# Five adds of squares in each feed forward's last group, from VectorE to GpSimd

## The chip, the cores and the metric

The kernel runs on one core of a Trainium2 chip. The core has five engines that work side by side and wait for each other by semaphores: TensorE (PE; matrix products, into the accumulator memory PSUM), VectorE (DVE), ScalarE (ACT), GpSimd (POOL), which also issues some of the DMAs, and SyncE (SP), which issues the others. The metric is the device time of one execution in microseconds (us), as the median of several runs; less is better.

## The reference, cut to what matters

One layer of a network over 512 positions and a width of 1024: a feed forward, a token mixer (attention) and a second feed forward, each behind an RMS norm, and a norm at the end.

```
def rmsnorm(x, g):
    x32 = x.astype(jnp.float32)
    y = x32 * lax.rsqrt(jnp.mean(x32 * x32, axis=-1, keepdims=True) + EPS)
    return (y * g.astype(jnp.float32)).astype(x.dtype)

def swiglu(x, w_gate, w_up, w_down):
    return (jax.nn.silu(x @ w_gate) * (x @ w_up)) @ w_down

x = x + 0.5 * swiglu(rmsnorm(x, ffn1_norm), ffn1_w_gate, ffn1_w_up, ffn1_w_down)
x = x + token_mixer(rmsnorm(x, mix_norm), w_in, w_out, ...)
x = x + 0.5 * swiglu(rmsnorm(x, ffn2_norm), ffn2_w_gate, ffn2_w_up, ffn2_w_down)
return rmsnorm(x, final_norm)
```

What the change touches is `mean(x32 * x32)`: the squares of x, summed over the width, which the norm of the mixer and the last norm need.

## The kernel before, in words

**Layout.** The activations lie transposed: x is eight tiles `x[0]` to `x[7]`, each of 128 of the 1024 columns (on the partitions) by 512 positions. All is float32. A product of two such matrices is made as three TensorE products of parts: each operand is split into a high part (a copy rounded to a shorter format, by ScalarE) and a low part (what the rounding left, a subtraction by VectorE), and high x high, high x low and low x high are added in PSUM (`mm3`, L123 to L126). So the weights also pass through ScalarE (`high`, L383) and VectorE (`low`, L387) before TensorE can use them.

**Squares.** `sq` (L90) is one tile of 128 x 512. It collects, over the eight tiles of x, the squares: the first tile's square is written to it, each of the others is squared into a scratch tile by ScalarE and then added to `sq`. TensorE later sums `sq` over the partitions (`means`, L177, and `final_means`, L1236). There are three places that add: `add_square` (L717, VectorE) at the start; `square_x` (L145, GpSimd, L151) after the mixer; and `squared` (L788, VectorE, L800) in the last group of both feed forwards, which is what changes.

**A feed forward** (`ffn`, L199) ends with its down product. Most of it is made by a recursive scheme of seven products for four blocks (`SEVEN`, L46), in units of two tiles of x. The last group's units are named ("d", 1, m) with m = 0, 2, 4, 6; each updates `x[m]` and `x[m+1]`. A unit has seven steps in the order a11, s3, s2, a12, s1, a22, s4, one product of twelve TensorE instructions each. `down_step` (L591) puts the updates of x from PSUM on VectorE (all printed as L424): s1 and s4 both use the bank `py`, s1's result being read by VectorE before s4 is added to it. For each step VectorE also makes a low part (L387), and for s2 and s4 a sum of weights (`total`, L365 and L367). The sums s1 and s3 of the weights are made by DMAs: SP loads one block, and GpSimd issues a DMA that adds the other (`weight_sums`, L331 to L340).

**Order.** In this stage the order of VectorE's, ScalarE's, GpSimd's and SP's instructions is fixed by hand: a list of events with due times in units of `STEP` (L55) is worked off in order of time (`pipeline`, L613), and each engine works its instructions off in that order. After steps a22 and s4 of a last group's unit, `ended` (L611) is called for x[m+1] and then x[m]. So x[1] comes first, then x[0], x[3], x[2], x[5], x[4], x[7], x[6]. In the first feed forward `ended` is `to_mixer` (L802): ScalarE makes the high part `xh`, then the square, and VectorE the add and the low part `xl` (L806), for the mixer's products. In the second it is `squared` alone, and the last unit (x[6], x[7]) goes another way (`last`, L1218; its squares are not added but summed by TensorE). So `squared` adds for m = 0, 2, 3, 4, 5, 6, 7 in the first feed forward and for m = 0, 2, 3, 4, 5 in the second: twelve adds; x[1] is squared straight into `sq`.

The scratch tiles `sqd` come from a pool of two buffers (tag "ptb", L796). Behind the first feed forward, some small work for the mixer is placed where there is room: a DMA on GpSimd's queue loads `lt` (L814), and VectorE reads it (L816); also the first weights of the mixer (L115, L116).

Of the kernel before, what the change touches and what calls it, by code (L numbers as in the profile page):

```python
# [18 lines left out]
ALU = mybir.AluOpType  # L19
# [35 lines left out]
STEP, PLAIN_STEP = 1410, 4080  # L55
# [10 lines left out]
def tile_macaron(ctx: ExitStack, tc, xs, xT, wf, wgu1, wst1, wd1, wdg1, wqk, wv, wo, wgu2, wst2, wd2,  # L66
                 wdg2, lams, relb, onehot, addc, out):
    nc = tc.nc
    V, A, G, T = nc.vector, nc.scalar, nc.gpsimd, nc.tensor
# [20 lines left out]
    sq = cp.tile([P, S], F32, tag="sq", name="sq")  # L90
# [697 lines left out]
    def squared(m, t, put):  # L788

        if m == 1:  # L790
            put(t + STEP, A.activation, sq[:], x[m], AF.Square)
            return
        sqt = {}

        def square():
            sqt[0] = tp.tile([P, S], F32, tag="ptb", name=f"sqd{m}")  # L796
            A.activation(sqt[0][:], x[m], AF.Square)

        put(t + STEP, square)
        put(t + 2 * STEP, lambda: V.tensor_tensor(sq[:], sq[:], sqt[0][:], op=ALU.add))  # L800

    def to_mixer(m, t, put):  # L802
        g = gain(1, m)
        put(t + STEP, lambda: A.activation(xh[m][:], x[m], AF.Copy, scale=g))
        squared(m, t, put)
        put(t + 2 * STEP, lambda: V.scalar_tensor_tensor(xl[m][:], x[m], g, xh[m][:].bitcast(F32),  # L806
                                                  op0=ALU.mult, op1=ALU.subtract))
# [33 lines left out]
    def put(t, rank, f, *a):  # L841
        at.setdefault(t, []).append((rank, f, a))
# [432 lines left out]
    def final_end():  # L1275
# [8 lines left out]
    means, spread = rstd("n3", n3)  # L1284
    ffn(wgu2, wst2, wd2, wdg2, EARLY[1], PAIRED[1], 2, early, n3, "b",
        {(0, 4): means, (0, 7): spread}, squared, last=last)


# [97 lines left out]
```

## Time and profile before

| what | us |
|---|---|
| median of 3 runs | 926.12 (926.03 to 926.28) |
| the profiled execution | 925.75 |
| its span, first to last instruction | 924.0 |
| TensorE busy | 911.2 |
| VectorE busy | 722.2 |
| ScalarE busy | 532.9 |
| GpSimd busy | 98.3 |
| the first feed forward's last group | 297.99 to 338.43 |
| the second feed forward's last group | 870.75 to 910.82 |

How to read the rows: PE, PEld, DVE, ACT, POOL and SP are the engines (PEld is TensorE's weight load). A row of a timeline has start (us from the span's start), duration in us, engine, line of the kernel, operation, output<-inputs by the program's names (buffer numbers left out), shapes and types, and how many instructions it stands for; in brackets the idle time of the engine before it and what ended it. In the names, a and b at the end stand for the first and the second feed forward (`pyda` is the bank y of a down unit of the first). The rows of instructions on one engine can overlap by some 0.08 us, since the next one is started while the last one ends; the time an instruction takes of a full queue is the distance from its start to the next start.

### The profile page before, as it was taken

What the parts mean: (1) busy time and instruction counts of PE and PEld (TensorE: products, weight loads), DVE (VectorE), ACT (ScalarE), POOL (GpSimd) and SP (SyncE); (2) the same over time, 40 slices, a digit from 0 to 9 for tenths busy, and PEclk for the clock granted to TensorE, in tenths of its full rate; (3) what the DMA queues carried; (4) which work ended last, traced back from release to release, by engine and by line L of the source; (5) the groups of instructions that cost most, each with busy time, mean ns of one, the idle gap of its engine ahead of it and who ended that gap; (6) DMA issues with size and microseconds to landing.
All of it is one profiled execution on the core that took longest, in us unless ns stands there. A gap on an engine that the chain in (4) does not pass through costs nothing.

```text
span 924.0 us, 17216 instructions
## 1 busy us (share of the span) xinstructions
PE 911.2 (99%) x6462; PEld 845.8 (92%) x6462; DVE 722.2 (78%) x1491; ACT 532.9 (58%) x1101; POOL 98.3 (11%) x117
## 2 busy tenths in 40 slices
PE   9999999999999999999999999999999999999995
PEld 7788999999999998988989888888999899999995
DVE  7697997687997994779764547697899678798796
ACT  7455774455764664666756655354676354667462
POOL 0011101012102100000000003201110102220100
PEclk9999999999999999999999999999999999999998
DMA  7176646578757732343333104445674757884732
GB/s 256 64 199 154 169 130 183 142 205 208 196 152 194 188 129 86 115 132 121 91 115 93 69 23 137 130 135 145 162 190 113 197 155 185 217 216 118 209 105 92
DMA packets 60388, 136.71 MB, mean 148 GB/s; under 512 B 6848, under 2 KB 9152, under 8 KB 60304
## 3 DMA queue, kind: packets, MB, share of 16 engines
q1 hardware_dynamic: 46304, 110.14, 36.2%
q0 software_dynamic: 14000, 25.47, 17.2%
q8 instruction: 50, 0.82, 0.4%
q14 instruction: 34, 0.28, 0.1%
HBM read 130.30 MB, written 2.14 MB: 143 GB/s over the span
## 4 chain that ended last, share of the span: by engine, by line
PE 93%; DVE 4%; ACT 1%; issue 1%; DMA 0%; SPq 0%; DVEq 0%; ACTq 0%
PE po L1052 2%; PE pv L902 2%; PE pv L904 2%; PE pv L903 2%; PE pwo L124 2%; PE pwo L125 2%; PE pwo L126 2%; PE pua L125 1%; PE pua L124 1%; PE pua L126 1%; PE pt L1036 1%; PE pda L125 1%; PE pdb L125 1%; PE pub L124 1%; PE pda L124 1%; PE pub L125 1%
## 5 line engine op out<-in xcount | busy, mean ns | idle before, releaser
L1015 DVE CUSTOM_DVE_ANT_0 pr<-sc,strip 128x128 f32<-128x128 f32 (+3 forms) x64 | 30.8, 487 | 30.6 <-PE sc L1013 30.2
L1018 ACT ACTIVATE pr<-pr,small 128x128 f32<-128x128 f32 (+3 forms) x64 | 36.0, 563 | 28.2 <-DVE small L1015 27.3
L383 ACT CAST w<-s2b 128x512 fp32r<-128x512 f32 x50 | 31.2, 625 | 20.6 <-DVE s2b L365 20.3
L383 ACT CAST w<-s2a 128x512 fp32r<-128x512 f32 x46 | 28.7, 625 | 21.7 <-DVE s2a L365 18.9
L151 POOL TENSOR_TENSOR sq<-sq,sqt 128x512 f32<-128x512 f32 x7 | 10.9, 1560 | 248.2 <-ACT sqt L150 248.2
L387 DVE TENSOR_TENSOR w<-s2b,w 128x512 fp32r<-128x512 f32 x50 | 34.4, 688 | 2.4 <-ACT w L383 2.0
L902 PE MATMUL pv<-w,xh 128*128 128x256 f32 x128 | 36.0, 281 | 0.0
L903 PE MATMUL pv<-w,xl 128*128 128x256 f32 x128 | 35.8, 280 | 0.0
L904 PE MATMUL pv<-w,xh 128*128 128x256 f32 x128 | 35.8, 280 | 0.0
L1052 PEld LDWEIGHTS po<-v,ptb 128*128 128x128 f32 x240 | 32.6, 191 | 2.5
L387 DVE TENSOR_TENSOR w<-s2a,w 128x512 fp32r<-128x512 f32 x46 | 31.6, 687 | 1.7 <-ACT w L383 1.3
L1052 PE MATMUL po<-v,ptb 128*128 128x64 f32 (+1 forms) x240 | 32.3, 268 | 0.0
L1042 ACT COPY ptb<-pt 128x128 f32<-128x128 f32 (+3 forms) x47 | 19.4, 420 | 16.4 <-PE pt L1036 16.0
L124 PE MATMUL pq<-xh,w 128*128 128x512 f32 x64 | 26.7, 416 | 0.0
L864 DVE TENSOR_TENSOR w<-raw_qk,w 128x512 fp32r<-128x512 f32 x32 | 21.7, 687 | 5.3 <-ACT w L860 5.3
L124 PE MATMUL pwo<-mh,w 128*128 128x512 f32 x64 | 25.6, 400 | 0.0
L125 PE MATMUL pq<-xl,w 128*128 128x512 f32 x64 | 25.1, 393 | 0.0
L124 PE MATMUL pk<-xh,w 128*128 128x512 f32 x64 | 25.1, 392 | 0.0
L126 PE MATMUL pq<-xh,w 128*128 128x512 f32 x64 | 25.1, 392 | 0.0
L125 PE MATMUL pwo<-ml,w 128*128 128x512 f32 x64 | 25.0, 391 | 0.0
L126 PE MATMUL pk<-xh,w 128*128 128x512 f32 x64 | 25.0, 391 | 0.0
L126 PE MATMUL pwo<-mh,w 128*128 128x512 f32 x64 | 25.0, 391 | 0.0
(672 smaller groups left out, 3974.3 us busy)
## 6 DMA issues: line engine op xcount, KB each, us to landing
raw_qk<-wqk_dram SPq DMA_DIRECT2D x16, 512.0 KB, 3.2
raw0bg<-wst_dram SPq DMA_DIRECT2D x9, 512.0 KB, 4.3
raw_gua<-wgu_dram SPq DMA_DIRECT2D x8, 512.0 KB, 4.0
raw0ag<-wst_dram SPq DMA_DIRECT2D x8, 512.0 KB, 4.6
raw0ad<-wdg_dram SPq DMA_DIRECT2D x8, 512.0 KB, 5.0
strip<-bias_rows SPq DMA_DIRECT2D x16, 256.0 KB, 3.6
raw_v<-wv_dram SPq DMA_DIRECT2D x8, 512.0 KB, 3.2
raw_wo<-wo_dram SPq DMA_DIRECT2D x8, 512.0 KB, 3.2
```

Source lines behind the costliest of these rows:

```text
L124: T.matmul(po, wh, mh, start=first, stop=False, skip_group_check=on)
L125: T.matmul(po, wh, ml, start=False, stop=False, skip_group_check=on)
L126: T.matmul(po, wl, mh, start=False, stop=last, skip_group_check=on)
L383: A.copy(made[t][0], source(t))
L387: V.tensor_tensor(l, source(t), h.bitcast(F32), op=ALU.subtract)
L864: V.tensor_tensor(l[:, c:c + 512], raw[:, c:c + 512], h[:, c:c + 512].bitcast(F32), op=ALU.subtract)
L902: T.matmul(po, xh[k][:, xs], wh[:, o:o + 256], start=k == 0, stop=False)
L903: T.matmul(po, xl[k][:, xs], wh[:, o:o + 256], start=False, stop=False)
L904: T.matmul(po, xh[k][:, xs], wl[:, o:o + 256], start=False, stop=k == KD - 1)
L1015: V.tensor_tensor_reduce(out=pi, in0=ps[:, :w], in1=st["b"][m][:, w - 1::-1], op0=ALU.add, op1=ALU.min, scale=1.0, scalar=3.0e38, accum_ou ...
L1018: A.activation(pi, pi, AF.Exp, scale=-1.0, bias=st["mx"][:, m, i:i + 1], accum_out=st["ls"][:, m, i:i + 1])
L1052: T.matmul(st["po3"][:, i, d0:d0 + dn], st["ptb", m, i][:, k * P:(k + 1) * P], vt[u // 4, k][:, fo + d0:fo + d0 + dn], start=k == 0, stop= ...
```

## The change

Of the adds in `squared`, those with m up to 5 go to GpSimd (`G`); those of m = 6 and 7 stay on VectorE (`V`). That is five in each feed forward (m = 0, 2, 3, 4, 5): in the second all that there are. Their place in the list of events is the same; on GpSimd they stand in its queue behind the DMAs of the last weight sums.

```
-        put(t + 2 * STEP, lambda: V.tensor_tensor(sq[:], sq[:], sqt[0][:], op=ALU.add))
+        put(t + 2 * STEP, lambda: (V if m > 5 else G).tensor_tensor(sq[:], sq[:], sqt[0][:], op=ALU.add))
```

## The prediction

> **What bounds the kernel now.** I read the page first, for the span, the engines and the chain of waits.
>
> ```profile
> span 924.0 us, 17216 instructions
> ...
> PE 911.2 (99%) x6462; PEld 845.8 (92%) x6462; DVE 722.2 (78%) x1491; ACT 532.9 (58%) x1101; POOL 98.3 (11%) x117
> ...
> PE 93%; DVE 4%; ACT 1%; issue 1%; DMA 0%; SPq 0%; DVEq 0%; ACTq 0%
> ...
> L151 POOL TENSOR_TENSOR sq<-sq,sqt 128x512 f32<-128x512 f32 x7 | 10.9, 1560 | 248.2 <-ACT sqt L150 248.2
> ```
>
> TensorE sets the time, and 4% of the chain is VectorE. VectorE's 78% is an average, so I cut out the units of the two last groups, where the change lies: the units m=2, 4, 6 of the first feed forward, and m=4 of the second. Columns: stretch, its length, busy time (count) of PE, PEld, DVE, ACT, POOL, clock, DMA share, GB/s.
>
> ```profile
> 309.06:318.58 9.52, 9.52 (x87) 9.52 (x85) 9.35 (x19) 6.88 (x15) 0.89 (x1) 1.00 0.93 242
> 318.58:328.23 9.65, 9.65 (x86) 9.62 (x85) 9.65 (x20) 6.71 (x14) 0.57 (x1) 1.00 0.32 101
> 328.23:338.43 10.20, 9.87 (x87) 9.67 (x86) 10.20 (x21) 8.50 (x16) 0.00 (x0) 1.00 0.30 106
> ...
> 889.88:899.40 9.52, 9.52 (x87) 9.52 (x86) 8.89 (x18) 5.96 (x13) 0.00 (x0) 1.00 0.08 29
> ```
>
> An undisturbed unit takes TensorE 9.52 us. In the first feed forward VectorE is busy for all 9.65 and all 10.20 us of the last two, and TensorE runs late (9.65, 10.20). In the second, VectorE has 0.63 us to spare in a unit, since it makes no `xl` there. Next, the chain and TensorE's own rows at the end of the first feed forward:
>
> ```profile
> 332.74 0.74 DVE xl L806
> ...
> 336.49 0.35 DVE x L424
> 336.88 0.39 PE pyda L124
> ```
>
> ```profile
> 325.38 0.28 PE L124 MATMUL pxda<-h5a,w 128*128 128x256 f32 x1
> ...
> 326.74 0.38 PE L124 MATMUL pyda<-h1a,w 128*128 128x256 f32 x1
> ...
> 335.03 0.28 PE L124 MATMUL pxda<-h5a,w 128*128 128x256 f32 x1
> ...
> 336.88 0.39 PE L124 MATMUL pyda<-h1a,w 128*128 128x256 f32 x1 [0.33 <-DVE x L424]
> ```
>
> A product takes 1.36 us (325.38 to 326.74). The last product of the last unit, s4, should have begun at 335.03 + 1.36 = 336.39 and began at 336.88. It adds into the bank py that s1 left, so it has to wait until VectorE has read py into `x` (L603, printed as L424), and that update stands in a queue without a gap:
>
> ```profile
> 309.26 0.42 DVE L424 SCALAR_TENSOR_TENSOR x<-pyda,x 128x256 f32<-128x256 f32 x1 [0.16 <-PE pyda L126]
> ...
> 316.25 0.42 DVE L424 SCALAR_TENSOR_TENSOR x<-pyda,x 128x256 f32<-128x256 f32 x1
> ...
> 319.72 0.68 DVE L800 TENSOR_TENSOR sq<-sq,sqd 128x512 f32<-128x512 f32 x1
> 320.32 0.75 DVE L806 SCALAR_TENSOR_TENSOR xl<-x,x,xh 128x512 fp32r<-128x512 f32 x1
> 320.98 0.68 DVE L367 TENSOR_TENSOR s2a<-raw0ad,s2a 128x512 f32<-128x512 f32 x1
> 321.58 0.69 DVE L387 TENSOR_TENSOR w<-s1ad,w 128x512 fp32r<-128x512 f32 x1
> ...
> 326.26 0.42 DVE L424 SCALAR_TENSOR_TENSOR x<-pyda,x 128x256 f32<-128x256 f32 x1
> ...
> 336.41 0.42 DVE L424 SCALAR_TENSOR_TENSOR x<-pyda,x 128x256 f32<-128x256 f32 x1
> ```
>
> The wait for TensorE at 309.26 is the last one on VectorE before 336.41. In this stretch each 0.1 us more on VectorE is 0.1 us more at 336.41, and hence at s4. All five moved adds of this feed forward (m = 0, 3, 2, 5, 4) lie in it.
>
> **The change part by part.** *Removed from VectorE:* an add occupies its queue for 320.32 - 319.72 = 0.60 us; five make 3.0 us in each feed forward.
>
> *Added to GpSimd:* the same add, and the kernel already has seven of that shape on GpSimd, made while VectorE works (rows of GpSimd, then of VectorE and ScalarE):
>
> ```profile
> 556.58 1.51 POOL L151 TENSOR_TENSOR sq<-sq,sqt 128x512 f32<-128x512 f32 x1 [230.12 <-ACT sqt L150]
> 558.29 1.49 POOL L151 TENSOR_TENSOR sq<-sq,sqt 128x512 f32<-128x512 f32 x1 [0.20 <-ACT sqt L150]
> 563.56 1.29 POOL L151 TENSOR_TENSOR sq<-sq,sqt 128x512 f32<-128x512 f32 x1 [3.78 <-ACT sqt L150]
> ```
>
> ```profile
> 553.73 0.68 DVE L116 TENSOR_TENSOR w<-raw_wo,w 128x512 fp32r<-128x512 f32 x1
> ...
> 556.19 0.74 DVE L138 SCALAR_TENSOR_TENSOR elb<-x,x,ehb 128x512 fp32r<-128x512 f32 x1
> 556.85 1.78 DVE L116 TENSOR_TENSOR w<-raw_wo,w 128x512 fp32r<-128x512 f32 x1
> 558.56 1.77 DVE L138 SCALAR_TENSOR_TENSOR elb<-x,x,ehb 128x512 fp32r<-128x512 f32 x1
> ```
>
> ```profile
> 555.88 0.62 ACT L150 ACTIVATE sqt<-x 128x512 f32<-128x512 f32 x1
> ```
>
> The add starts 0.08 us after ScalarE's square ends (555.88 + 0.62 = 556.50, start 556.58). GpSimd being slow (1.29 to 1.51 us) would not matter; what matters is that VectorE's next instruction takes 1.78 us where its like takes 0.68, and the one after 1.77 where its like takes 0.74. Both end just over 0.5 us after the add in front of them ended (556.58 + 1.51 = 558.09, then 558.63; 559.78, then 560.33). So VectorE stands still while GpSimd adds. Each add costs VectorE 1.03 to 1.10 us and saves it 0.60: a net loss of 0.43 to 0.50.
>
> Bounds for one add, from rows: at best no block, -0.60; at worst its longest record, 1.51 us, less 0.60, +0.91. I take +0.46, because the two rows are the same add against the same two shapes of VectorE work (`w` and `xl`/`el` subtractions, both inputs in SBUF) in a queue without gaps. In the units at stake the add's place is followed by instructions of the same kind, two operands in SBUF, for nearly 2 us (320.32 to 322.27), so an add there meets one.
>
> The Trainium skill, "SBUF — State Buffer", section "Who interferes with whom", says more than the rows: of VectorE with two SBUF inputs and GpSimd reading SBUF, the one that starts second is blocked for the first one's whole instruction. Taken with the shortest record, 1.29 us, that would be +0.69 an add and +3.45 us in all, 929.6; the rows show a block of 1.03 to 1.10, and I go by them.
>
> *How it reaches TensorE, first feed forward.* After the add of m=0 the update at 316.25 ends 0.46 later, 317.13; its s4 is due one product ahead of the next unit, at 318.58 - 1.36 = 317.22, so nothing yet. After m=3 and m=2 the lateness is 3 x 0.46 = 1.38: the update at 326.26 ends at 328.06, and s4, due at 326.74, begins some 1.4 us late. After m=5 and m=4 it is 5 x 0.46 = 2.3, and the s4 of 336.88 begins at 339.2. The next stage's products follow without a gap, so its end moves by the same. The weights' low parts, also queued behind a blocked instruction, are made a product ahead, and TensorE is already late by then; they add nothing. ScalarE's squares wait for a buffer of two, whose earlier add is long done.
>
> *Second feed forward.* Two adds a unit are again 0.92 us net on VectorE, but here it waits for TensorE:
>
> ```profile
> 896.88 0.42 DVE L424 SCALAR_TENSOR_TENSOR x<-pydb,x 128x256 f32<-128x256 f32 x1 [0.34 <-PE pydb L126]
> ...
> 902.34 0.69 DVE L800 TENSOR_TENSOR sq<-sq,sqd 128x512 f32<-128x512 f32 x1
> ...
> 904.75 0.70 DVE L387 TENSOR_TENSOR w<-s2b,w 128x512 fp32r<-128x512 f32 x1 [0.44 <-ACT w L383]
> ...
> 906.72 0.42 DVE L424 SCALAR_TENSOR_TENSOR x<-pxdb,x 128x256 f32<-128x256 f32 x1 [0.95 <-PE pxdb L126]
> ```
>
> ```profile
> 898.04 0.28 PE L124 MATMUL pydb<-h1b,w 128*128 128x256 f32 x1
> ```
>
> In the unit m=4 the cover is 0.34 idle before the update and 898.04 - 897.30 = 0.74 after it, 1.08 us against 0.92. In the last unit it is 0.44 + 0.95 = 1.39. The last add, now some 1.5 us later than 902.34 + 0.69, is still ahead of 906.72, and the means that read `sq` come later. So I take 0 here; without the cover, 0.9 us a unit.
>
> *Queues.* GpSimd's DMAs for the last weight sums are issued ahead of the adds; behind or between them comes only the load of `lt`:
>
> ```profile
> 325.89 0.57 POOL L814 DMA_DIRECT2D lt<-lams_dram  x1 [15.94 <-DVE x L424]
> ```
>
> ```profile
> DMA to landing us min/median/max: 3.2/3.2/3.2
> ```
>
> ```profile
> 335.61 0.28 DVE L816 TENSOR_TENSOR lp<-lt 128x128 f32<-128x128 f32 x1
> ```
>
> ```profile
> 330.83 0.62 ACT L797 ACTIVATE sqd<-x 128x512 f32<-128x512 f32 x1
> ```
>
> It lands at 325.89 + 3.2 = 329.1, over 6 us before VectorE reads it at 335.61, and is expected to stay ahead of the last adds (the last row is the square of m=4); 0 in the sum.
>
> *Sum.* The profiled execution took 925.75 us (span 924.0), 0.37 below the median of the runs. 925.75 + 2.3 = 928.05; on the median 926.12 + 2.3 = **928.4 us**.
>
> **The rivals.**
> *B, part of the block is hidden.* The updates of `x` read PSUM and only one SBUF operand; no row shows one beside a GpSimd add. If the adds fall beside them, or the lag of 0.46 is made up while VectorE waits for a stalled TensorE, about half of the loss goes: +1.1, **927.2**. Against it: the work behind an add's place (320.32 to 321.58) has two operands in SBUF. The Trainium skill's same section says that a VectorE instruction with at most one SBUF input does not contend; no run here shows it, and it would give this rival.
>
> *C, not slower: VectorE is relieved as the work moved suggests.* At the end of the first feed forward, its 3.0 us are freed and no block replaces them, if GpSimd fits its adds between VectorE's instructions. TensorE then regains what it lost to late updates, 0.49 at 336.88 and 9.65 - 9.52 = 0.13 in the unit before: -0.6, **925.5**. It decides if VectorE's instructions beside the adds stay below 0.68 + 0.60 us. The two rows with 1.77 and 1.78 speak against it.
>
> *D, the order around the seam turns worse.* `lt` could fall behind the add of m=4 in GpSimd's queue. That square, ended at 331.45 before, ends near 332.9 when all is 1.4 late; with block, add and issue it lands close to 338, when VectorE reaches its reader (335.61 + 2.3 = 337.9). Or two low parts of the next stage's weights (0.60 each) slip in front of the last update, one is there already. Up to +1.2 more, **929.6**. For it: VectorE's order there is not fixed by hand beyond the feed forward's own work.
>
> **How the numbers follow.** Chances: forecast 0.68, B 0.13, C 0.06, D 0.13. The forecast's own range is 927.7 to 929.2 (five times 0.43 or 0.50, some rest of slack, a longer block). Reaching into B and D, 927.0 to 929.8 holds 8 in 10. A measurement tells 0.2%, 1.85 us, from no change: slower means above 927.97. That holds in about 0.85 of the forecast and nearly all of D, 0.58 + 0.12 = 0.70; the same is the rest of the forecast, B and most of C, 0.27; faster 0.03.
>
> **What would show it.** In the new profile: ten L800 adds on GpSimd of 1.3 to 1.8 us; behind each, one VectorE instruction of about 1.7 instead of 0.7 us; VectorE without a gap from 309 to about 339; s4 in unit m=4 beginning some 1.4 us late with a wait for L424, the last s4 2.3 late; from there the same lag to the end; the second feed forward's units still 9.52 us. I am wrong if VectorE's instructions keep their lengths, if the lag at the first feed forward's end is under 1 us or if the second loses time too.

## The result, and the profile after

| | us, median | executions |
|---|---|---|
| kernel before | 926.08 | 925.93 to 926.54, six |
| changed kernel | 930.73 | 928.52, 930.4, 930.62, 930.83, 930.97, 932.14 |

The ratio is 1.0048 (95% interval 1.0035 to 1.0061): slower, as forecast, but by twice as much as forecast and beyond the range. Two things are to be explained: why the profiled execution, 928.52, lies so near the forecast of 928.4, and why the other five are some 2 us longer, where those of the kernel before agree within 0.6. Five later executions of the changed kernel, `after_long` below, have their median at 929.13.

The page of the changed kernel's profiled execution:

```profile
span 926.8 us, 17226 instructions
...
PE 911.9 (98%) x6462; PEld 846.1 (91%) x6462; DVE 725.6 (78%) x1481; ACT 532.9 (57%) x1101; POOL 114.7 (12%) x127
...
PE 92%; DVE 5%; issue 1%; ACT 1%; DMA 0%; SPq 0%; DVEq 0%; ACTq 0%
```

VectorE has ten instructions fewer and is busy 3.4 us more. Its rows in the first feed forward's last group, all whose length changed, with the rows of GpSimd's adds after them:

```profile
315.13 1.35 DVE L365 TENSOR_TENSOR s2a<-s1ad,raw0ad 128x512 f32<-128x512 f32 x1
...
319.81 1.80 DVE L806 SCALAR_TENSOR_TENSOR xl<-x,x,xh 128x512 fp32r<-128x512 f32 x1
...
322.14 1.78 DVE L387 TENSOR_TENSOR w<-s1ad,w 128x512 fp32r<-128x512 f32 x1
...
330.72 1.81 DVE L806 SCALAR_TENSOR_TENSOR xl<-x,x,xh 128x512 fp32r<-128x512 f32 x1
...
333.06 1.78 DVE L387 TENSOR_TENSOR w<-s1ad,w 128x512 fp32r<-128x512 f32 x1
```

```profile
312.30 3.63 POOL L800 TENSOR_TENSOR sq<-sq,sqd 128x512 f32<-128x512 f32 x1 [2.99 <-ACT sqd L797]
319.77 1.29 POOL L800 TENSOR_TENSOR sq<-sq,sqd 128x512 f32<-128x512 f32 x1 [3.84 <-ACT sqd L797]
321.88 1.49 POOL L800 TENSOR_TENSOR sq<-sq,sqd 128x512 f32<-128x512 f32 x1 [0.81 <-ACT sqd L797]
...
330.69 1.28 POOL L800 TENSOR_TENSOR sq<-sq,sqd 128x512 f32<-128x512 f32 x1 [3.16 <-ACT sqd L797]
332.64 1.65 POOL L800 TENSOR_TENSOR sq<-sq,sqd 128x512 f32<-128x512 f32 x1 [0.66 <-ACT sqd L797]
```

Four adds block VectorE by 1.05 to 1.10 us each, as the two adds of the mixer did that the prediction reads (1.03 to 1.10). The mixer's other five meet a VectorE with gaps in its queue: one blocks it by 0.76 us, one not at all, and in the last three it is GpSimd that is held up (1.78 us for its add). The first add here, of m=0, blocks VectorE by 1.35 - 0.68 = 0.67 only, and late. The units of the group (stretch, length, then busy times, as in the prediction), three of the first feed forward and the unit m=4 of the second:

```profile
309.15:318.67 9.52, 9.52 (x87) 9.52 (x86) 9.35 (x18) 6.82 (x15) 3.79 (x2) 1.00 0.92 249
318.67:329.25 10.58, 9.79 (x87) 9.59 (x86) 10.58 (x18) 6.77 (x14) 3.38 (x3) 1.00 0.26 82
329.25:341.16 11.91, 9.89 (x87) 9.68 (x85) 11.81 (x24) 8.66 (x16) 2.93 (x2) 1.00 0.39 117
892.59:902.11 9.52, 9.52 (x87) 9.52 (x86) 9.36 (x16) 5.78 (x13) 3.14 (x2) 1.00 0.10 29
```

The first feed forward's units were 9.52, 9.65 and 10.20 us; the second's is 9.52 as before. TensorE's waits in front of the two last s4:

```profile
327.78 0.38 PE L124 MATMUL pyda<-h1a,w 128*128 128x256 f32 x1 [0.79 <-DVE x L424]
...
339.69 0.38 PE L124 MATMUL pyda<-h1a,w 128*128 128x256 f32 x1 [2.02 <-DVE x L424]
```

VectorE's queue ahead of the last read of py:

```profile
337.30 0.68 DVE L116 TENSOR_TENSOR w<-raw_v,w 128x512 fp32r<-128x512 f32 x1
337.90 0.41 DVE L424 SCALAR_TENSOR_TENSOR x<-pwda,x 128x256 f32<-128x256 f32 x1
338.23 0.28 DVE L816 TENSOR_TENSOR lp<-lt 128x128 f32<-128x128 f32 x1
338.43 0.68 DVE L116 TENSOR_TENSOR w<-raw_v,w 128x512 fp32r<-128x512 f32 x1
339.03 0.27 DVE L818 TENSOR_REDUCE ls<-lp 128x2 f32<-128x128 f32 x1
339.23 0.41 DVE L424 SCALAR_TENSOR_TENSOR x<-pyda,x 128x256 f32<-128x256 f32 x1
```

That read starts at 339.23, in the kernel before at 336.41: 2.82 us later, of which 0.09 were there at the group's start (its first product begins at 298.08 against 297.99). The rest splits into the blocks less 0.60 each, 0.07 + 0.45 + 0.49 + 0.47 + 0.50 = 1.98, and a second part that is no block: the order in which the mixer's first work was fitted in (the seam, as the texts below call this place). Ahead of the read there now stand two L116, L816 and L818, 1.6 us by their distances, where L816 and one L116, 0.8 us, stood before. Together 1.98 + 0.80 = 2.78 us, against the 2.73 that were to be split.

### The profile page after: what moved, and what is told of

Read it like the earlier page. It is cut to its first block, busy times and chain, and to the rows that moved or that the text cites. A ratio compares the mean times of both kernels' runs of the same rounds, so it can differ in the third digit from the quotient of the medians.

```text
span 926.8 us, 17226 instructions
## 1 busy us (share of the span) xinstructions
PE 911.9 (98%) x6462; PEld 846.1 (91%) x6462; DVE 725.6 (78%) x1481; ACT 532.9 (57%) x1101; POOL 114.7 (12%) x127
## 4 chain that ended last, share of the span: by engine, by line
PE 92%; DVE 5%; issue 1%; ACT 1%; DMA 0%; SPq 0%; DVEq 0%; ACTq 0%
PE po L1052 2%; PE pv L902 2%; PE pv L903 2%; PE pv L904 2%; PE pwo L124 2%; PE pwo L125 2%; PE pwo L126 2%; PE pua L125 1%; PE pua L124 1%; PE pua L126 1%; PE pt L1036 1%; PE pdb L125 1%; PE pda L125 1%; PE pub L125 1%; PE pdb L126 1%; PE pda L126 1%
```

## The experiments

All times are medians with their range, unless single executions are listed; each kernel was timed beside the kernel before on its own chip (925.9 to 926.1 us).

**Where the loss is: one feed forward at a time.** In `first_only` the condition is `G if first and m <= 5 else V` (with `first` handed over by `to_mixer`), in `second_only` `V if first or m > 5 else G`. Theory 1 of the texts below puts the loss and its spread down to the adds of the first feed forward, theory 2 puts the spread, and what lies over 928.5 us, down to the second.

> The five adds on GpSimd in the first feed forward only; VectorE makes those of the second. Theory 1: about 930.7 us with the same spread of executions, as the whole change. Theory 2 (the spread and the part over 928.5 come from the second feed forward): 928.5 to 929 us, executions within 0.5 us of each other.

> The five adds on GpSimd in the second feed forward only. Theory 1 (covered by VectorE's waits for TensorE there): 926.1 us, within 0.5 of the kernel before. Theory 2: 928 to 929 us, with spread.

| | us | executions |
|---|---|---|
| first_only | 928.85 | 928.39, 928.75, 928.85, 930.11, 930.46 |
| second_only | 926.33 | 926.16 to 927.34, ten |

The second feed forward costs nothing that can be measured (ratio 1.0004, 0.9994 to 1.0013), the first all that shows (1.0035, 1.0022 to 1.0048), executions over 930 us included. Below, the executions near 928.5 us are called the lower heap and those near 930 us and above the upper one. The whole change, on the chip of these two runs, took 928.82 us in its one execution (`after_look1`). Theory 2 falls. The cover is there in the second feed forward's rows; VectorE's, then GpSimd's, of the changed kernel:

```profile
892.78 0.42 DVE L424 SCALAR_TENSOR_TENSOR x<-pydb,x 128x256 f32<-128x256 f32 x1 [0.16 <-PE pydb L126]
893.13 1.55 DVE L387 TENSOR_TENSOR w<-raw0bd,w 128x512 fp32r<-128x512 f32 x1
```

```profile
892.83 1.30 POOL L800 TENSOR_TENSOR sq<-sq,sqd 128x512 f32<-128x512 f32 x1 [5.93 <-ACT sqd L797]
```

They also answer a question of rival B. The update at 892.78 reads PSUM and one SBUF operand; it runs beside the add for 0.37 us and keeps its 0.42. The low part behind it, two SBUF operands, waits. That is what the section of the Trainium skill cited in the prediction ("SBUF — State Buffer", "Who interferes with whom") says of an instruction with one SBUF input; the rival failed since no such update stood behind the four later adds of the first feed forward. Not every update is of this kind: those behind s3 read two SBUF operands, x and `rbc_n`.

**What blocks: the adds left out, and GpSimd writing only.** The edit of `no_adds`, and of `write_only`:

```
+        if m > 5:
+            put(t + 2 * STEP, lambda: V.tensor_tensor(sq[:], sq[:], sqt[0][:], op=ALU.add))
...
+        else:
+            put(t + 2 * STEP, lambda: [G.memset(sqt[0][:], 0.0) for i in range(2)])
```

> The ten moved adds are made by no engine, so the two norms behind miss the squares of x[0], x[2], x[3], x[4] and x[5]. If VectorE's relief is worth what TensorE lost to late updates in the first feed forward (0.6 us) and GpSimd's adds are the whole loss: 925.4 us. If the loss of the change lies in the order of VectorE's work at the seam (low parts of the mixer's weights ahead of the last update), this kernel keeps about 0.9 us of it and is not faster than 926.1.

> In place of each of the ten moved adds GpSimd writes zeros over the scratch tile twice, in the same place of its queue; the norms behind miss the squares of x[0], x[2], x[3], x[4] and x[5]. GpSimd reads nothing. If VectorE is blocked by GpSimd's reading (theory of the shared read path): no VectorE instruction longer than 0.8 us beside it, 925.4 us as without the adds. If any work of GpSimd blocks VectorE: instructions of 1.2 us and more, 927 us and above.

| | us | executions |
|---|---|---|
| no_adds | 925.38 | 924.77 to 925.60, nine, and one 929.01 |
| write_only | 925.28 | 925.15 to 925.66, ten |

Both leave the ten adds out, and both come out at the price worked out for VectorE's relief (925.4 and, in rival C, 925.5), though the interval of `no_adds` reaches no change (0.9995, 0.9986 to 1.0005; `write_only` 0.9989, 0.9980 to 0.9998). With GpSimd writing 128x512 twice beside VectorE's subtractions, VectorE keeps its lengths. GpSimd's row of `write_only`, then VectorE's:

```profile
319.96 1.11 POOL L803 MEMSET sqd<- 128x512 f32 x2 [6.05 <-ACT sqd L797]
```

```profile
319.73 0.68 DVE L387 TENSOR_TENSOR w<-raw0ad,w 128x512 fp32r<-128x512 f32 x1
320.33 0.74 DVE L809 SCALAR_TENSOR_TENSOR xl<-x,x,xh 128x512 fp32r<-128x512 f32 x1
```

So it is GpSimd's reading, not its being busy, that stops VectorE.

**The first add.** In `first_m0` only the add of m=0 goes to GpSimd, in `first_no_m0` those of m = 2 to 5; `first_warm` is first_only with one add of the same size on GpSimd at the program's start.

> In the first feed forward only the add of m=0 is on GpSimd, VectorE makes all others. Theory 1a (GpSimd's first add of the program starts late, some 2.3 us, by its own first use, and takes VectorE's path when it is ready; it costs about 0.1 us net): 926.2 us. Theory 1b (this add's varying time is what spreads the executions by 2 us): 926 to 928 us, with a spread that the kernel before lacks.

> In the first feed forward the adds of m=3, 2, 5 and 4 are on GpSimd, that of m=0 on VectorE. Four blocks of 1.1 us less 0.60 each, and the seam's order: 928.5 us. Theory 1a: some of the first add's late start shows now at m=3. Theory 1b: executions within 0.5 us of each other, no 930s. If the 930s stay, they come from the four later adds or from the seam.

> As the adds on GpSimd in the first feed forward only, plus one add of 128x512 on GpSimd at the very start, into a tile that is loaded later. Theory 1a: the add of m=0 now takes about 1.3 us instead of 3.6 and blocks VectorE by 1.1 instead of 0.7: profiled execution about 929 us. If the late start comes from the arbitration with VectorE, the 3.6 us stay. If the first use is what differs between executions, all executions agree within 0.5 us.

| | us | executions |
|---|---|---|
| first_m0 | 925.97 | 925.65 to 927.07, ten |
| first_no_m0 | 929.67 | 928.58 to 930.30, ten |
| first_warm | 929.98 | 928.57 to 931.20, ten |

The add of m=0 alone is free (0.9998, 0.9988 to 1.0007), and the spread is there without it: theory 1b falls. Its 3.6 us stay with the early add, so theory 1a's first use is not the reason; in `first_m0` too the add takes 3.62 us and blocks one instruction for 0.67. Being the first add behind GpSimd's DMAs isn't it either: in `first_no_m0` that is the add of m=3, and it takes 1.39 us; and the two writes of `write_only` in the place of m=0 take 1.11 us as everywhere. So it belongs to an add in this place, and why it is late there is open.

The profile of `first_warm` (its profiled execution took 930.00 us) gave the clue to the spread: behind the last wait TensorE's step takes 2.25 us, where the changed kernel's profiled execution has 1.47. Its stretches of 2 us there (length, then busy times of PE, PEld, DVE, ACT and POOL, granted clock, DMA share, GB/s):

```profile
340.00:342.00 2.00, 2.00 (x12) 2.00 (x12) 1.19 (x6) 1.30 (x3) 0.00 (x0) 0.59 0.79 260
342.00:344.00 2.00, 2.00 (x13) 2.00 (x12) 1.69 (x5) 1.72 (x4) 0.00 (x0) 0.56 0.01 2
```

The granted clock is 0.59 and 0.56. From this came theory 3: TensorE's wait of 2.0 us makes the clock fall in part of the executions.

**The wait and the clock.** `fill` (on first_only) and `after_fill` (on the changed kernel) give TensorE something to do in the wait:

```
+ if nm == "a" and u == units[-1] and o[0] == "s4":
+     for i in range(16):   # after_fill: 12
+         T.matmul(banks["z"], h[:, :P], moving(u, o[2])[0][0], start=True, stop=True, ...)
```

`before_wait` makes such a wait without GpSimd, in the kernel before, by making the low part of s4 three times:

```
- at(starts[t] - 3 * STEP, 2.5, low, t)
+ for i in range(3 if nm == "a" and t == len(ops) - 1 else 1): at(starts[t] - 3 * STEP, 2.5, low, t)
```

`after_look1`, `after_look2`, `after_look3` and `after_long` are the changed kernel again.

> The changed kernel again, for a second profile: its profiled execution was 928.52 us, its other five 930.4 to 932.1. Theory 1 (what differs between executions is who gets the shared path at the five adds of the first feed forward: in the profiled one the add of m=0 lost, took 3.63 us and blocked VectorE by 0.67 us only): a slower execution shows the last s4 of the first feed forward over 2.7 us late against the kernel before, and nothing added later. Theory 2 (the second feed forward loses in the slower executions): the lag at the first feed forward's end is 2.7 us again and grows by about 2 us between 870 and 915 us.

> The adds on GpSimd in the first feed forward only, and ahead of the last s4 of that feed forward sixteen more products of 128x256 on TensorE, into the bank z, which nobody reads any more. They fill 1.8 of the 2.0 us in which TensorE waits there. Theory 3 (in part of the executions this wait makes the granted clock fall to about 0.57 for 3.4 us, which costs 1.6 us more): with TensorE kept busy the fall does not come, all executions at 928.4 to 929.0 us, none at 930 or above. If the spread has another cause, some executions stay at 930 and above.

> The changed kernel again, beside the next one on the same chip, to see how its executions are spread: theory 3 (an occasional fall of the clock after the 2.0 us wait) has them in two heaps, near 928.6 and near 930.3 us, most in the upper one. If the profiled execution falls in the upper heap, its clock falls below 0.7 between 340 and 344 us.

> The whole change, with twelve products of 128x256 into the unread bank z ahead of the last s4 of the first feed forward, 1.4 of the 2.0 us of TensorE's wait there. Theory 3: all executions at 928.5 to 929.5 us, none at 930 or above. If the twelve do not keep the clock up, or the spread has another cause: executions at 930 and above as in the changed kernel.

> The kernel before, no add on GpSimd, but in the first feed forward's last unit VectorE makes the low part for s4 three times over. With the order that follows at the seam, 2.4 us stand ahead of the last read of py where 0.8 stood: TensorE's wait before the last s4 grows to about 2 us, as long as in the changed kernel. Theory 3 (the wait alone makes the granted clock fall in part of the executions): two heaps, near 926.1 + 1.6 = 927.7 and near 929.3 us. If the upper heap of the changed kernel comes from GpSimd and VectorE meeting on the shared path: one heap at 927.7, within 0.6 us.

> The changed kernel, one more profile. Theory 3: if it took over 930 us, the granted clock falls below 0.7 for some 3.4 us behind TensorE's 2.0 us wait at 340 us; if it took 928.5 to 929.2, it does not.

> As the run before: over 930 us with the clock falling behind the 2.0 us wait, or 928.5 to 929.2 without.

| | us | executions |
|---|---|---|
| after_look1, 2, 3 | 928.82, 930.16, 930.73 | one each |
| after_long | 929.13 | 928.86, 928.92, 929.13, 929.67, 930.47 |
| fill | 929.16 | 929.02 to 929.49, five |
| after_fill | 929.45 | 929.10 to 929.80, five |
| before_wait | 928.04 | 927.75 to 928.34, six; 929.26, 929.92, 930.02 |

`before_wait` shows both heaps without any add on GpSimd, 1.3 to 2 us apart, and its profile fell in the upper one. First TensorE's row with the wait, then the same view of stretches:

```profile
339.19 0.39 PE L124 MATMUL pyda<-h1a,w 128*128 128x256 f32 x1 [1.93 <-DVE x L424]
```

```profile
338.00:340.00 2.00, 0.81 (x6) 0.81 (x7) 2.00 (x6) 0.50 (x1) 0.00 (x0) 0.94 0.44 150
340.00:342.00 2.00, 2.00 (x11) 2.00 (x11) 1.37 (x4) 1.98 (x3) 0.00 (x0) 0.50 0.28 113
342.00:344.00 2.00, 2.00 (x15) 2.00 (x13) 1.90 (x7) 1.99 (x6) 0.00 (x0) 0.70 0.81 262
344.00:346.00 2.00, 2.00 (x20) 2.00 (x19) 1.97 (x6) 0.43 (x1) 0.00 (x0) 1.00 0.01 4
```

The changed kernel itself, in `after_look3` (930.73 us), the same two views:

```profile
340.39 0.39 PE L124 MATMUL pyda<-h1a,w 128*128 128x256 f32 x1 [2.00 <-DVE x L424]
```

```profile
340.00:342.00 2.00, 1.61 (x10) 1.61 (x11) 1.81 (x8) 0.90 (x3) 0.00 (x0) 0.77 0.56 158
342.00:344.00 2.00, 2.00 (x11) 2.00 (x11) 1.15 (x4) 1.78 (x5) 0.00 (x0) 0.50 0.26 104
344.00:346.00 2.00, 2.00 (x17) 2.00 (x16) 2.00 (x6) 1.55 (x4) 0.00 (x0) 0.87 0.00 0
```

and the profiled execution of 928.52:

```profile
340.00:342.00 2.00, 2.00 (x20) 2.00 (x19) 1.71 (x10) 1.39 (x3) 0.00 (x0) 1.00 0.83 262
342.00:344.00 2.00, 2.00 (x20) 2.00 (x19) 2.00 (x6) 2.00 (x5) 0.00 (x0) 1.00 0.00 0
```

A stretch of 2 us holds 20 matmuls at full clock and 11 at 0.50. In `after_look3` the last s4 takes 2.19 us instead of 1.47, and the 37 matmuls behind it 5.22 instead of 4.31: 1.6 us. With the wait filled no execution of ten is above 929.8. That is weaker than it looks, since on the chip of `after_fill` the unfilled kernel passed 930 in one of five only (`after_long`), and on that of `fill` in two of five (`first_only`); and the fillers cost some 0.6 us of their own (532.6 to 532.7 us from this group's end to the second feed forward's last group, instead of 532.0 to 532.1), as more of the mixer's small work was fitted in ahead of x[6] and x[7], and the mean behind waits 0.36 us for them.

The Trainium skill, "TensorE: Matmul & The Clock Gate", section "What's actually happening", tells of a clock that halves after an idle window of about 3.4 us, the window running on by itself. The fall to 0.50 agrees with that; the wait that is enough is shorter here, 1.93 to 2.02 us. That only part of the executions show the fall would fit a window that runs on by itself, but no run here shows the window. Of the seven profiles with a wait of 1.93 to 2.02 us, three show the fall (`first_warm`, `before_wait`, `after_look3`) and four don't.

Not all of the upper heap is the clock. `after_look2` took 930.16 us at a clock of 1.00 throughout this stretch:

```profile
340.00:342.00 2.00, 0.81 (x7) 0.82 (x8) 2.00 (x7) 0.42 (x2) 0.00 (x0) 1.00 0.21 59
342.00:344.00 2.00, 2.00 (x20) 2.00 (x19) 1.71 (x9) 1.90 (x4) 0.00 (x0) 1.00 0.61 246
```

Its last group began at 299.58, 1.5 us later than in the profiled execution of 928.52 (298.08), some of it already at the first weights. The profile of `first_no_m0` (929.82 us) is the same case, with its last group at 299.58 and no fall, and that of `after_long` (929.67 us, 298.97) has no fall either. So of the six profiles over 929.5 us three show the fall, and the longest without it is 930.16. What makes the start late, and how often, wasn't tried. It needs no add on GpSimd: of the 101 executions of the kernel before in all runs four took over 927 us (927.05, 927.40, 928.77 and 930.15), and one of `no_adds` 929.01.

Each timed execution has its mean granted clock on record, and 3.4 us at 0.50 of some 927 lower it by 0.002. The 167 executions of kernels without a long wait before the last s4 have 0.994 to 0.996. Of the 48 of kernels with it, 24 of the 27 over 929.2 us have 0.994 or less, and only 7 of the 21 below; the four at 0.992 or 0.993 are all in the upper heap. So most of the upper heap has the fall by these figures, but a single execution at 0.994 can be either.

**The seam's order, in both kernels.** The mixer's first work on VectorE (L816 to L826, and the low parts of the first two weight tiles) is kept behind the read of py after s1, `seam[0]` being that instruction:

```
+    behind.enter_context(tc.issue_after(seam[0].ins))
...
+    with tc.issue_after(seam[0].ins):
+        prep(0, True), prep(1, True)
```

> The adds on GpSimd in the first feed forward only, with VectorE's work for the mixer (the low parts L116, L816, L818) kept behind the last read of py after s1. In the first profile these took 0.68 + 0.28 + 0.68 + 0.27 us ahead of it, pitch 1.6 in all. Theory (the seam's order is part of the loss, and a wait of under 1 us leaves the clock alone): TensorE's wait there falls from 2.0 to under 1 us, 927.0 to 927.5 us, no executions at 930. If the order costs nothing: 928.5 to 930.5 as before.

> The kernel before, VectorE making all adds, with the same order at the seam: two instructions (L816, L116, 0.8 us) no longer stand ahead of the last read of py. The last s4 loses its wait of 0.33 to 0.5 us: 925.6 us. If the work behind it (the low parts for the mixer's first products, the mean) becomes late instead: 926.1 us or more.

| | us | ratio to before |
|---|---|---|
| first_seam | 927.43 (927.28 to 928.17, eleven) | 1.0016 (1.0007 to 1.0025) |
| before_seam | 925.53 (925.06 to 926.02, eleven) | 0.9993 (0.9984 to 1.0002) |

VectorE's queue in the profile of `first_seam`, with the read of py now ahead of all that work:

```profile
337.93 0.40 DVE L424 SCALAR_TENSOR_TENSOR x<-pyda,x 128x256 f32<-128x256 f32 x1
338.26 0.27 DVE L816 TENSOR_TENSOR lp<-lt 128x128 f32<-128x128 f32 x1
338.46 0.67 DVE L116 TENSOR_TENSOR w<-raw_v,w 128x512 fp32r<-128x512 f32 x1
```

With the order held, the same five adds cost 1.3 us instead of the 2.8 of `first_only`, no wait of TensorE there is over 0.8 us, and there is no upper heap: the order and the clock were over half of the loss. The same edit on the kernel before makes 925.53, the lowest median of a version with all of the work in it: 0.6 us less, but the interval still reaches no change, so that it is faster isn't shown.

## Why the prediction was partly right

- *The price of an add* was right. The four later adds block 1.05 to 1.10 us where 1.03 to 1.10 was read, and that reading is what blocks is shown by `write_only`. (The bound at worst was misread: the longest of the mixer's seven records is 1.78 us, not 1.51, but in those GpSimd was the one that waited.) The add of m=0 was put at +0.46 and costs +0.07: it held up one instruction in part. Just ahead of that instruction, at 314.79, stood an update that reads PSUM; if the add read from about then on, that explains it, but when it read isn't shown. Without adds, the median lies at rival C's price of the relief (925.38).
- *How it reaches TensorE* was right in place: s4 of the unit m=4, then the last s4, both waiting for the read of py. The lag at the first was worked out as 1.4 us; by the unit's ends it is 329.25 - 328.23 - 0.09 = 0.93, mainly for the first add. At the end 2.3 was expected and 341.16 - 338.43 - 0.09 = 2.64 came.
- *The second feed forward* costs nothing, as the cover of 1.08 and 1.39 us said (`second_only` 926.33).
- *GpSimd's queue*: `lt`, at 326.94, stayed ahead of the last adds and came in time.
- *The order at the seam* was put into rival D and left out of the sum. It came, 0.80 us, by its second arm: one more low part, and L818, ahead of the last read.
- *The near hit is in part luck.* The profiled execution, 928.52, had no fall of the clock, and two errors went against each other: the first add cost 0.39 less than the sum has, the order 0.80 more. Profile against profile the sum says 928.05, which is 0.47 too little; it looks nearer because the kernel before was profiled in an execution 0.37 below the median.
- *The step that failed* is "the next stage's products follow without a gap, so its end moves by the same". The 2.3 us were carried on as a plain shift at full clock. The runs show that a wait of 2.0 us makes the clock fall to 0.50 in part of the executions, and this adds 1.6 us behind it; and that the shift itself was 2.64, with the seam's order that the sum left out. By the sum, 2.64 + 1.6 = 4.2 us over the kernel before, 930.3. The five timed executions lie at 930.4 to 932.1, above it and above any profile without the fall (930.16), so the fall is likely in most of them. It isn't shown for each: their mean granted clock is 0.994, and so is that of the profiled execution, which has no fall. What lies over 930.3, up to 1.8 us, stays open; a late start of the last group, 1.5 us in two profiles, is one candidate. So does why five of six executions here took over 930 us, and three of the eight in the later runs.

## What to carry to other kernels

In this kernel, moving two-operand work from VectorE to GpSimd costs nothing only where VectorE has idle time to be blocked in: the price is 1.1 us of block for 0.6 us of work. When a stall is predicted on TensorE, its length decides as well as its sum: here a wait of 0.79 us cost just that, and one of 2.0 us cost 3.6 in part of the executions. And work that a scheduler fits in around a fixed order can land ahead of the one instruction that the bound engine waits for, so that order is worth fixing first.

## What was not expected

- A wait of 1.93 to 2.02 us is enough for the granted clock to fall to 0.50 for some 3.4 us, but not each time: in 3 of the 9 timed executions of `before_wait`, by their times (two of them have the lowest mean granted clock of that run, 0.992).
- The add of m=0 takes 3.63 us in the profiled execution of the changed kernel and 3.62 in `first_only`, `first_m0` and `first_warm`, with no block for the first 2.5 us; an earlier add doesn't change it.
- In some executions TensorE's steps behind the 0.79 us wait take 1.41 to 1.44 us instead of 1.36, at a granted clock of 1.00 (`after_long`, `after_look2`, `first_seam`). Behind VectorE this cost nothing; its reason is open.
